# A two-layer hybrid decoder on one core: S5 kernel tables made with swapped operands in four column groups, and the first block's table work emitted later

## Chip, cores, metric

The kernel runs on one core of a Trainium2 chip. The metric is the time of one execution on the device in microseconds, the median of several runs.

## What is computed

256 tokens of width 1024 pass two layers. Each layer has a token mixer of three branches (attention, a spatial gating unit, an S5 state space model), then a feed-forward part: a dense SwiGLU in the first layer, a top-2 of 8 mixture of experts in the second. The S5 branch is the one that is changed here:

```python
dt = jnp.exp(log_dt)[:, None]
lam_bar = jnp.exp(lam * dt)
b_bar = ((lam_bar - 1.0) / lam)[..., None] * b
bu = jnp.einsum('gpi,btgi->btgp', b_bar, u)
_, states = lax.associative_scan(combine, (a, bu), axis=1)
y = jnp.real(jnp.einsum('gip,btgp->btgi', c, states)) + d_skip * u
...
y_c = gelu(y)
y_c = y_c * sigmoid(y_c @ w_glu + b_glu)
```

## The kernel before

Weights stream from HBM and are split on chip into a high and a low part (`wh` on ScalarE, `wl` on VectorE, lines 202 and 203); every product of the dense part is three matmuls, lines 297 to 299. The program is a list of units. A unit is 24 such matmuls for most weights (about 2.9 us of TensorE), and the mixer's list is, in order: zv, v, u, q, k, zu (four units each from u on, here k1 to k4, zu1 to zu4), 24 gate units `gt` (g1 to g24), four units p1 (the gating unit's output projection, tile `pp`), two units wg (tile `pg`, the S5 branch's GLU), p0, p2, and the output projection. After the first layer's mixer come the dense FFN's units, then the second layer's mixer, then the experts.

Between units a planner (`Side`, lines 126 to 171) puts in pieces of the branch work. It runs at build time and settles the order of each engine's instructions; an engine executes in that order and waits where an operand isn't there. The work stands in four lanes of Python generators: P (S5 constants and tables, then `s5_prep`, block by block), A (`s5`: the scans), C (gating unit), B (attention). A positive yield is a cost, a negative one a hold on the lane in units' time. `stream` adds `u.us * rate` to a credit (2.57 x 1.4 in the mixer) up to 3.0, takes 1.13 off for every weight split (made three units ahead) and a further 0.6 for each p1 unit, and gives the rest to `advance` behind the unit's matmuls:

```python
    def advance(self, budget, us):                       # line 151
        for k in self.hold:
            self.hold[k] -= us
        spent = 0.0
        while spent < budget:
            live = [k for k, q in self.lanes.items() if q and self.hold[k] <= 0]
            ...
            spent += self._step(min(live, key=PRIO.index))   # PRIO = "ACPB"
```

A unit can name work that must be whole before it (`pre`): `units[-2].pre = (f"s5{l}",)`, line 1060, names S5 for the first wg unit. `stream` then calls `finish` (lines 163 to 171), which emits all that is left of it, whatever the holds, ahead of the unit's matmuls.

S5 is done in four blocks of 128 channels for each layer. `s5_block` (P) makes a block's tables: VectorE writes the input table into `SB` (`cm`, lines 645 to 658), TensorE transposes it (`pt`, line 680) and ScalarE copies it to `bt`; VectorE writes `SC`; then TensorE multiplies `SB` with the padded output coefficients `cp4` (from GpSimd, lines 664 to 671) and adds the skip term: `kk`, lines 687 to 691. Seven ScalarE copies (lines 694, 698) place parts of `kk` in `ST`. There is one `SB`, while `SC` and `ST` exist twice, so a block from the third on waits until the scan two blocks before it is done. `s5_scan` (A) then does a block: `pp` (line 711), a copy to `vt` (718), 14 VectorE instructions (722 to 741), a hold of 3.5, `py` (748 to 751), a copy into U (752). After the fourth block `s5` applies GELU (538), holds 4.0, reorders with a matmul (548, tile py2), copies (551) and splits the result into `gh` and `gl`, which the wg units read. `s5_u` (line 594, tile `pu`) reorders the input before the first block. In layer 0 blocks are made while the mixer runs, and `s5_prep` starts at k1. In layer 1 they are made during the dense FFN and spilled to HBM, and loaded again when the second mixer begins.

Of the kernel before, what the change touches and what calls it, by code (L numbers as in the profile page):

```python
# [14 lines left out]
AF = mybir.ActivationFunctionType  # L15
# [158 lines left out]
class K:  # L174
# [455 lines left out]
    def s5_block(self, l, b, bc):  # L630
        nc = self.nc
        V = nc.vector
        q = slice(16 * l + 4 * b, 16 * l + 4 * b + 4)
        SC, ST = self.SC[b % 2], self.ST[b % 2]
        pr_ = self.g4("s5p")
        t1, t2 = (pr_[:, 256 * i:256 * i + 256].rearrange("p (q m i) -> p q m i", q=4, m=4) for i in range(2))
        cnp = pr_[:, 512:768].rearrange("p (k q i) -> p k q i", k=2, q=4)

        def cm(dst, coef, yr, yi, neg):
            d4 = [dst[:, 512 * i:512 * i + 512].rearrange("p (q m h i) -> p q m h i", q=4, m=4, h=2)  # L640
                  for i in range(2)]
            xr, xi = (z[:, :, q].rearrange("p m q -> p q m")[:, :, :, None].to_broadcast([128, 4, 4, 16])
                      for z in coef)
            yr, yi = (z[:, :, None, :].to_broadcast([128, 4, 4, 16]) for z in (yr, yi))
            V.tensor_tensor(t1, yr, xr, op=OP.mult)
            V.tensor_tensor(t2, yi, xi, op=OP.mult)
            for h in range(2):
                s = slice(64 * h, 64 * h + 64)
                V.tensor_tensor(d4[0][s, :, :, h], t1[s], t2[s], op=OP.subtract)
            yield 1.4  # L650
            V.tensor_tensor(t1, yr, xi, op=OP.mult)
            V.tensor_tensor(t2, yi, xr, op=OP.mult)
            for h in range(2):
                s = slice(64 * h, 64 * h + 64)
                if neg:
                    V.scalar_tensor_tensor(d4[1][s, :, :, h], t1[s], -1.0, t2[s], op0=OP.mult, op1=OP.subtract)
                else:
                    V.tensor_tensor(d4[1][s, :, :, h], t1[s], t2[s], op=OP.add)
            yield 1.4

        bre, bim, cre, cim = (bc[:, 64 * i:64 * i + 64].rearrange("p (q i) -> p q i", i=16) for i in range(4))

        cp4 = self.sp.tile([128, 3, 4, 32], F32, tag="cpad", name="cpad", bufs=1)
        nc.gpsimd.memset(cp4, 0.0)
        for h in range(2):
            s = slice(64 * h, 64 * h + 64)
            nc.gpsimd.tensor_copy(cp4[s, 0, :, 16 * h:16 * h + 16], cre[s])
            nc.gpsimd.tensor_scalar(cp4[s, 1, :, 16 * h:16 * h + 16], cim[s], -1.0, None, op0=OP.mult)
        d = self.cst[:, C_D + 16 * l + 4 * b:C_D + 16 * l + 4 * b + 4, None]
        nc.gpsimd.tensor_tensor(cp4[:, 2], self.ident[:, None, 96:128].to_broadcast([128, 4, 32]),  # L670
                                d.to_broadcast([128, 4, 32]), op=OP.mult)
        yield from cm(self.SB, self.GT, bre, bim, False)
        yield -2.5

        bt = self.g4("bt")
        for i in range(2):
            pt = self.ax("pt")
            for j in range(4):
                s = slice(512 * i + 128 * j, 512 * i + 128 * j + 128)
                nc.tensor.transpose(pt[:, 128 * j:128 * j + 128], self.SB[:, s], self.ident)  # L680
            nc.scalar.activation(bt[:, 512 * i:512 * i + 512], pt, AF.Copy)
            yield 0.1
        yield from cm(SC, self.LT, cre, cim, True)
        yield -2.5

        kk = self.ax("kk")
        nc.tensor.matmul(kk[:, 0:128], self.ident, cp4[:, 2].rearrange("p q i -> p (q i)"), start=True, stop=False)
        for j in range(4):
            o = kk[:, 32 * j:32 * j + 32]
            nc.tensor.matmul(o, self.SB[:, 128 * j:128 * j + 128], cp4[:, 0, j], start=False, stop=False)  # L690
            nc.tensor.matmul(o, self.SB[:, 512 + 128 * j:512 + 128 * j + 128], cp4[:, 1, j], start=False, stop=j == 3)
        t4 = ST.rearrange("p (q l i) -> p q l i", l=4, i=32)
        kk3 = kk[:, 0:128].rearrange("p (q i) -> p q i", i=32)
        nc.scalar.activation(t4[:, :, 3], kk3, AF.Copy)
        for lo in range(3):
            for m in range(lo + 1):
                s = 3 - lo + m
                nc.scalar.activation(t4[32 * m:32 * m + 32, :, lo], kk3[32 * s:32 * s + 32], AF.Copy)
        yield 0.1
        return bt  # L700
# [1127 lines left out]
```

## Time and profile before

| | us |
|---|---|
| median of 3 runs (1605.46 to 1605.67) | 1605.63 |
| the profiled execution | 1605.73 |
| its span, first to last instruction | 1603.8 |
| TensorE busy | 1552.4 (97%) |
| VectorE busy | 1026.7 (64%) |
| ScalarE busy | 781.9 (49%) |
| mean granted TensorE clock | 0.987 |

The times of the runs are the device's for one execution; the span is that of the instructions inside the profiled one. Layer 0's mixer lies between 7 and 270 us, the dense FFN up to 474, layer 1's mixer behind it, and from about 720 us on the experts. In a timeline row stand the start, the duration, engine, line and operation, output and inputs, shapes, how many are joined in the row, and in brackets how long the engine was idle before and what it waited for. Two records of a float32 matmul are its two passes.

### The profile page before, as it was taken

The numbers are of one execution on the slowest core, as the hardware profiler recorded it, in microseconds if no ns is written. First come the engines' busy times: TensorE is split into PE (matmuls) and PEld (weight loads), VectorE is DVE, ScalarE is ACT, GpSimd is POOL, SyncE is SP. The second block draws the span as 40 slices with busy tenths as digits, with TensorE's granted clock in tenths as the row PEclk, the third lists the DMA queues.
The fourth block names the chain that finished last, engine by engine and source line by source line (L and its number), as shares of the span: only waits on it lengthen the run. The fifth ranks groups of instructions, "written<-read, shape, count | busy, mean of one in ns | idle before, by whom it ended". The sixth has DMA issues, their size and how long they took to land. (4 is left out here: it accounts for less than half of the span.)

```text
span 1603.8 us, 24314 instructions
## 1 busy us (share of the span) xinstructions
PE 1552.4 (97%) x9175; PEld 1178.0 (73%) x9175; DVE 1026.7 (64%) x1501; ACT 781.9 (49%) x1081; POOL 139.0 (9%) x226
## 2 busy tenths in 40 slices
PE   7899999999999999988999999999999999999995
PEld 6899997999879999976766665565665666566551
DVE  7987778687563675667865564655665565565533
ACT  5355564355534557425654454554553554454530
POOL 2621000631001110010000000000000000000000
PEclk9999999999999999998999999999999999999997
DMA  8333356466755534586899999999999999999992
GB/s 328 134 134 130 106 190 244 158 229 232 286 206 215 195 129 164 193 328 240 342 409 397 415 416 413 415 415 415 414 415 415 414 416 415 415 411 415 415 414 113
DMA packets 90045, 487.29 MB, mean 304 GB/s; under 512 B 10128, under 2 KB 10144, under 8 KB 50752
## 3 DMA queue, kind: packets, MB, share of 16 engines
q1 hardware_dynamic: 83376, 462.46, 73.1%
q0 software_dynamic: 6544, 23.20, 4.1%
q8 instruction: 74, 1.21, 0.3%
q14 instruction: 51, 0.42, 0.1%
HBM read 477.23 MB, written 8.39 MB: 303 GB/s over the span
## 5 line engine op out<-in xcount | busy, mean ns | idle before, releaser
L1512 PE MATMUL gu<-moe_u,xes 128*64 128x512 f32 x400 | 165.1, 597 | 0.0
L1512 PE MATMUL gu<-moe_g,xes 128*64 128x512 f32 x400 | 165.0, 597 | 0.0
L203 DVE TENSOR_TENSOR wl<-moe_d,wh 128x1024 fp32r<-128x1024 f32 x112 | 132.6, 1220 | 49.9 <-ACT wh L202 39.5
L203 DVE TENSOR_TENSOR wl<-moe_g,wh 128x1024 fp32r<-128x1024 f32 x112 | 132.0, 1221 | 33.3 <-ACT wh L202 30.6
L203 DVE TENSOR_TENSOR wl<-moe_u,wh 128x1024 fp32r<-128x1024 f32 x112 | 133.9, 1221 | 25.1 <-ACT wh L202 19.4
L202 ACT ACTIVATE wh<-moe_u 128x1024 fp32r<-128x1024 f32 x112 | 116.3, 1058 | 19.5 <-PE moe_g L307 13.8
L202 ACT ACTIVATE wh<-moe_g 128x1024 fp32r<-128x1024 f32 x112 | 116.2, 1058 | 18.4 <-PE da L307 12.3
L202 ACT ACTIVATE wh<-moe_d 128x1024 fp32r<-128x1024 f32 x112 | 113.2, 1052 | 11.7 <-DMA moe_d<-moe_d 7.1
L297 PE MATMUL gt<-XTH,wh 128*128 128x256 f32 x384 | 111.2, 290 | 0.0
L298 PE MATMUL gt<-XTL,wh 128*128 128x256 f32 x384 | 108.5, 283 | 0.0
L299 PE MATMUL gt<-XTH,wl 128*128 128x256 f32 x384 | 108.5, 283 | 0.0
L1512 PEld LDWEIGHTS gu<-moe_g,xes 128*64 128x64 f32 x400 | 46.7, 137 | 78.2 <-issue 74.5
L202 ACT ACTIVATE thl<-pht 128x512 fp32r<-128x512 f32 x28 | 16.7, 597 | 158.9 <-PE pht L1538 158.4
L306 PE MATMUL moe_g<-wh,xeh 128*128 128x512 f32 x224 | 90.9, 406 | 0.0
L306 PE MATMUL da<-wh,thl 128*128 128x512 f32 x224 | 90.5, 404 | 0.0
L307 PE MATMUL moe_u<-wl,xeh 128*128 128x512 f32 x224 | 87.4, 390 | 1.4 <-DVE wl L203 1.4
L307 PE MATMUL moe_g<-wl,xeh 128*128 128x512 f32 x224 | 87.8, 392 | 0.1
L306 PE MATMUL moe_u<-wh,xeh 128*128 128x512 f32 x224 | 87.5, 391 | 0.0
L307 PE MATMUL da<-wl,thl 128*128 128x512 f32 x224 | 87.4, 390 | 0.0
L308 PE MATMUL da<-wh,thl 128*128 128x512 f32 x224 | 87.4, 390 | 0.0
L308 PE MATMUL moe_g<-wh,xel 128*128 128x512 f32 x224 | 87.2, 389 | 0.0
L308 PE MATMUL moe_u<-wh,xel 128*128 128x512 f32 x224 | 87.2, 389 | 0.0
(507 smaller groups left out, 4049.2 us busy)
## 6 DMA issues: line engine op xcount, KB each, us to landing
moe_g<-moe_g SPq DMA_DIRECT2D x68, 1024.0 KB, 12.5
moe_u<-moe_u SPq DMA_DIRECT2D x68, 1024.0 KB, 12.5
moe_d<-moe_d SPq DMA_DIRECT2D x68, 1024.0 KB, 13.5
gt<-w_st SPq DMA_DIRECT2D x24, 1024.0 KB, 4.8
moe_d<-moe_d SPq DMA_DIRECT2D x44, 512.0 KB, 12.2
fw<-ffn_gu SPq DMA_DIRECT2D x18, 1024.0 KB, 4.9
moe_u<-moe_u SPq DMA_DIRECT2D x34, 512.0 KB, 10.5
moe_g<-moe_g SPq DMA_DIRECT2D x34, 512.0 KB, 10.2
```

The source lines that it names most:

```text
L202: self.nc.scalar.activation(h, src, AF.Copy)
L203: self.nc.vector.tensor_tensor(l, src, h.bitcast(F32), op=OP.subtract)
L297: mm(o, wh[:, s], xh[:, x], start=k == 0, stop=False)
L298: mm(o, wh[:, s], xl[:, x], start=False, stop=False)
L299: mm(o, wl[:, s], xh[:, x], start=False, stop=k == nk - 1)
L306: mm(o, xh[:, xs[k]], wh[:, ws[k]], start=first and k == 0, stop=False)
L307: mm(o, xh[:, xs[k]], wl[:, ws[k]], start=False, stop=False)
L308: mm(o, xl[:, xs[k]], wh[:, ws[k]], start=False, stop=last and k == n - 1)
L1512: nc.tensor.matmul(box[0][o:o + 64], x[0][:, 64 * k:64 * k + 64], w[:, 512 * j:512 * j + 512], start=k == 0, stop=k == 7)
```

## The change

`kk` was the product with `SB` as stationary operand (128 columns loaded) and `cp4` as moving one (32 columns). Now `cp4` is stationary (32 columns) and `SB`, or the identity for the skip term, is moving (128 columns); the four groups of states go to four column groups of the array, 32 output partitions each. The result is the transpose of what is wanted, so ScalarE copies it into the unused end of the block's scratch tile and TensorE transposes it back, after a hold of 1.3, into another part of the same PSUM tile. In layer 0's first block alone, the hold ahead of `pt` goes from 2.5 to 7.0 and the hold ahead of `kk` from 2.5 to 5.0.

```diff
         yield from cm(self.SB, self.GT, bre, bim, False)
-        yield -2.5
+        yield -2.5 if l or b else -7.0
...
         yield from cm(SC, self.LT, cre, cim, True)
-        yield -2.5
-
-        kk = self.ax("kk")
-        nc.tensor.matmul(kk[:, 0:128], self.ident, cp4[:, 2].rearrange("p q i -> p (q i)"), start=True, stop=False)
-        for j in range(4):
-            o = kk[:, 32 * j:32 * j + 32]
-            nc.tensor.matmul(o, self.SB[:, 128 * j:128 * j + 128], cp4[:, 0, j], start=False, stop=False)
-            nc.tensor.matmul(o, self.SB[:, 512 + 128 * j:512 + 128 * j + 128], cp4[:, 1, j], start=False, stop=j == 3)
+        yield -2.5 if l or b else -5.0
+
+
+        kt = self.ax("kk")
+        for i in range(3):
+            for j in range(4):
+                w = self.ident if i == 2 else self.SB[:, 512 * i + 128 * j:512 * i + 128 * j + 128]
+                nc.tensor.matmul(kt[32 * j:32 * j + 32, 0:128], cp4[:, i, j], w, start=i == 0, stop=i == 2)
+        kts = pr_[:, 768:896]
+        nc.scalar.activation(kts, kt[:, 0:128], AF.Copy)
+        yield 0.1
+        yield -1.3
+        kk = kt[:, 128:256]
+        nc.tensor.transpose(kk, kts, self.ident)
         t4 = ST.rearrange("p (q l i) -> p q l i", l=4, i=32)
-        kk3 = kk[:, 0:128].rearrange("p (q i) -> p q i", i=32)
+        kk3 = kk.rearrange("p (q i) -> p q i", i=32)
```

## Rows read from the trace of the kernel before

**Rows 1.** Page: span; TensorE's busy tenths in 40 slices of it.
```profile
span 1603.8 us, 24314 instructions
...
PE   7899999999999999988999999999999999999995
```

**Rows 2.** TensorE's waits, 0 to 480 us: total us, times, longest.
```profile
PE pt L680 <- DVE S L649: 3.2, 1, 3.2
```

**Rows 3.** Busy by window: PE, PEld, DVE, ACT, POOL, granted clock, DMA share, GB/s.
```profile
70.00:80.00 10.00, 4.01 (x26) 3.60 (x26) 9.77 (x10) 1.18 (x3) 9.59 (x11) 0.84 0.00 0
```

**Rows 4.** TensorE's timeline from the end of k to the first zu unit.
```profile
71.37 0.28 PE L299 MATMUL k<-XTH,wl 128*128 128x256 f32 x1
74.88 0.63 PE L680 MATMUL pt<-ident,S 128*128 128x128 f32 x4 [3.23 <-DVE S L649]
78.27 1.12 PE L680 MATMUL pt<-ident,S 128*128 128x128 f32 x4 [2.76 <-DVE S L658]
...
79.40 0.42 PE L298 MATMUL zu<-XTL,wh 128*128 128x256 f32 x1
...
83.67 0.30 PE L297 MATMUL zu<-XTH,wh 128*128 128x256 f32 x1
```

**Rows 5.** VectorE's timeline: first block's product, zu's splits, second block's product.
```profile
69.69 1.27 DVE L645 TENSOR_TENSOR s5p<-s5par,GT 128x256 f32<-128x256 f32 x1
...
78.25 2.40 DVE L203 TENSOR_TENSOR wl<-zu,wh 128x1024 fp32r<-128x1024 f32 x2
...
92.35 0.46 DVE L645 TENSOR_TENSOR s5p<-s5par,GT 128x256 f32<-128x256 f32 x1
```

**Rows 6.** TensorE's timeline around the first block's table product.
```profile
87.86 0.28 PE L299 MATMUL zu<-XTH,wl 128*128 128x256 f32 x1
87.97 0.39 PE L687 MATMUL kk<-cpad,ident 128*128 128x128 f32 x2
...
90.10 0.28 PE L298 MATMUL zu<-XTL,wh 128*128 128x256 f32 x1
```

**Rows 7.** TensorE's timeline around `pu`, four column groups of 32.
```profile
52.04 0.28 PE L299 MATMUL q<-XTH,wl 128*128 128x256 f32 x1
...
52.25 1.93 PE L594 MATMUL pu<-uS,ident 128*32 128x256 f32 x32
...
54.33 0.28 PE L298 MATMUL q<-XTL,wh 128*128 128x256 f32 x1
```

**Rows 8.** TensorE's timeline around the third block's eight transpose passes.
```profile
148.10 0.28 PE L299 MATMUL gt<-XTH,wl 128*128 128x256 f32 x1
148.22 1.03 PE L680 MATMUL pt<-ident,S 128*128 128x128 f32 x8
...
149.22 0.28 PE L298 MATMUL gt<-XTL,wh 128*128 128x256 f32 x1
```

**Rows 9.** ScalarE's timeline: fourth block's `vt`, U and GELU.
```profile
191.30 0.60 ACT L718 ACTIVATE vt<-pp 128x512 f32<-128x512 f32 x1
...
208.34 0.37 ACT L752 ACTIVATE U<-py 128x256 f32<-128x256 f32 x1
...
210.02 1.06 ACT L538 ACTIVATE U<-U 128x1024 f32<-128x1024 f32 x1
```

**Rows 10.** VectorE's timeline: fourth block's scan, first and last step; `gl`.
```profile
191.93 0.42 DVE L724 TENSOR_TENSOR tq<-vt,ct 128x256 f32<-128x256 f32 x1
...
198.74 0.42 DVE L741 TENSOR_TENSOR vt<-tq 128x256 f32<-128x256 f32 x1
...
215.90 1.23 DVE L203 TENSOR_TENSOR gl<-yc,gh 128x1024 fp32r<-128x1024 f32 x1 [0.29 <-ACT gh L202]
```

**Rows 11.** TensorE's timeline: fourth block's `py`, py2, the first reader of `gl`.
```profile
202.55 0.33 PE L748 MATMUL py<-U,S 128*128 128x64 f32 x2
...
211.71 1.93 PE L548 MATMUL py<-U,ident 128*32 128x256 f32 x32
...
217.48 0.28 PE L298 MATMUL pg<-gl,wh 128*128 128x256 f32 x1
```

## The prediction

> **What bounds the kernel now.** I read the head of the page first: TensorE is busy eight tenths or more of every slice of the span but the first and the last [rows 1], so a microsecond taken from or put before TensorE in the two mixers or the dense FFN is a microsecond of the whole. Then TensorE's list of waits over the first 480 us: the S5 transposes `pt` stand in it [rows 2], and between 85 and 260 us it has no wait at all. The window of 70 to 80 us shows what happens at that place [rows 3]: TensorE works 4.01 of 10 us, VectorE and GpSimd nearly all of it, and the granted clock is down to 0.84 on the mean. TensorE's timeline there [rows 4] shows three losses: 3.23 us until the first four passes of `pt`, 2.76 us until the other four, and then half speed (1.2 of 2.4 GHz: matmuls 0.41 us long instead of 0.28) up to 83.67 us.
>
> Without them the first unit of zu would have begun at 71.49 (last k matmul 71.37 + 0.12) + 0.88 (eight `pt` passes, below) = 72.4 us; its 22nd matmul would have started 21 x 0.12 = 2.5 us later, at 74.9. It started at 83.67. So the place costs 8.8 us in all, and that is the most that later emission can give back.
>
> **Part 1, the table product.** Before, one block's `kk` is 18 records (9 fp32 matmuls of two passes each), every one with its own load of 128 weight columns, 0.11 us apart on the mean. From the last zu matmul ahead of it (87.86) to the second one behind it (90.10) is 2.24 us [rows 6]; two ordinary steps of 0.12 would be there anyway, so `kk` costs 2.0 us of TensorE, in each of eight blocks.
> The new form is 12 matmuls, 24 passes, of 128 moving columns into four column groups of 32. The trace has this form with 256 columns, in `pu` [rows 7]: 32 passes from 52.25 to 54.33 less the step behind, 2.29 - 0.24 = 2.05 us counted in the same way. A lone 128-column fp32 pass takes 0.11 us: eight transposes `pt` add 1.12 - 0.24 = 0.88 us [rows 8], so a 256-column pass would take 0.22, and 32 of them one by one 7 us. They took 2.05: four run side by side, 8 sets x 0.216 = 1.73, and 0.32 for entering and leaving this form. With 128 columns I take 6 sets x 0.108 + 0.32 = 0.97 us. The added transpose is two passes, 0.22. Saving per block: 2.0 - 0.97 - 0.22 = 0.81 us, in eight blocks 6.5 us. Bounds: if a set doesn't get shorter with fewer columns, 6 x 0.216 + 0.32 + 0.22 = 1.84, saving 1.3 us in all; if the change of form costs nothing, 9.1 us. I take the middle because a pass's time followed its columns [rows 7, 8]. One after another (2.6 + 0.2 us, a loss) is excluded [rows 7].
> The Trainium skill ("TensorE: Matmul & The Clock Gate", section "Wait - 56ns, not 53.3ns?") speaks against this: it says that without hardware decode the sequencer spends about 62 ns on every matmul, however small. By that 24 passes would take 1.5 us and the saving would be near 0.2 us a block, an estimate from that page; by it `pu` would take 2.0 us, and its 32 passes, over within 1.93 us with the last one's end [rows 7], speak against it but not by much.
> The copy `kts` on ScalarE is one more small activation a block, and the transpose stands one unit (2.9 us of TensorE) later, so ScalarE hides it as long as it is less than a unit behind; if not, the price is part of a microsecond at that block. In the FFN blocks nothing else hangs on it: the spilled tables are read over thirty units later.
>
> **Part 2, the first block later.** The planner counts in units: after each unit's matmuls `advance` takes 2.57 off every hold and spends a budget of at most 3.0 - 1.13 = 1.87 on lanes in the order A, C, P, B. A hold of 2.5 or 1.3 thus lasts one unit, 5.0 two, 7.0 three. I went through the units with these numbers (zu1 to zu4, then gate units g1 to g24, then p1-1 to p1-4, then wg1). For the kernel before, this count gives `pt` behind k4, `kk` behind zu2, the last block's `py` behind p1-1, `py2` behind p1-3: so it stands in the trace [rows 4, 6, 11]. As block: pt, kk, pp, py:
> before 0: k4, zu2, zu3, g3; 1: g3, g6, g7, g11; 2: g12, g14, g15, g19; 3: g18, g20, g21, p1-1.
> after 0: zu2, g1 (transpose g3), g4, g8; 1: g8, g12 (g13), g14, g18; 2: g17, g19 (g20), g21, p1-1; 3: g24, p1-2 (p1-3), p1-4, and `py` no longer before wg1.
>
> At the first block: zu1 now follows k4 at once, 71.49 to 74.4, then the attention scores. But zu2 needs its low half `wl`, and VectorE does that only behind the S5 product for this block, at 78.25 + 1.2 = 79.45 [rows 5]. That product is slow because GpSimd is busy then (1.27 us for what takes 0.46 at 92 us [rows 5]), which the change doesn't touch. So a wait for `pt` becomes a wait of some 4 us for `wl`. Then zu2's 22 other matmuls to 82.1 and `pt` to 83.0; before, both were done at 87.98 [rows 6]. Gain 5.0 us if the clock stays, 3.0 if it falls as it did before (20 steps took 4.27 us instead of 2.4 [rows 4]). I take 3.5; bounds 2 and 8.8.
>
> **Part 3, what comes due too early.** `wg1` may not start before S5 is done (`pre`). Before, its inputs were only just there: `gl` ended at 215.90 + 1.23 = 217.13, the matmul that reads it started at 217.48 [rows 10, 11]. After, the fourth block's `pp` stands behind p1-4, the last unit ahead of wg1, and `finish` puts the rest of S5 in front of wg1. TensorE executes in order, so it waits out this chain:
> - `vt` copy 0.60 [rows 9];
> - the scan on VectorE from 191.93 to 198.74 + 0.42 = 7.2 us, with one weight split in it, as there will be after [rows 10];
> - the rest of `py`, 20 of 24 passes at 0.11 [rows 6] and the last one's end: 2.5;
> - copy of U and GELU with its table load, 208.34 to 211.08: 2.7 [rows 9];
> - `py2` 1.93 [rows 11];
> - copies, `gh`, `gl`: at most 217.13 - 213.64 = 3.5 [rows 10, 11]; one weight split stood in it, I take 3.0.
> Sum 17.9. TensorE had to do `py` (24 x 0.11 = 2.7) and `py2` (2.05) anyway, so it idles 13.2 us, 13.5 with the `mg` product of p1-4 that VectorE does in the same queue. It idles 7 us at a stretch, longer than before the clock's fall above [rows 4], so the clock falls: `py` at half speed +2.1, `py2` +1.7, the start of wg1 +1.9, as 4.27 less 2.4 above. I take 4.5 of these 5.7. Loss 18.0 us, bounds 13.2 and 19.5. Nothing gives it back: behind it come units on which TensorE is busy without waits.
> Layer 1's reload begins at m1[0], over thirty units behind the last spill, so its chain doesn't move.
>
> **Sum.** Profiled execution 1605.73 (span 1603.8 + 1.9 around it; the median of the runs is 0.1 lower): -6.5 - 3.5 + 18.0 = +8.0, so 1613.7, against the median 1613.6 us.
>
> **Rivals.**
> A, faster: S5 of layer 0 still reaches `gh` ahead of wg1. Then part 3 is nothing and the time is 1605.6 - 10.0 = 1595.6. It decides at one point: `py` of block 3 must stand two units before wg1 (the hold of 4.0 ahead of `py2`). For it: the lanes share one budget, and attention ends three units earlier in my count. Against: the count, which fits the trace of before at every place I compared.
> B, the product isn't cheaper: the sets of four stay at 0.216, the saving is 1.3 us and the time 1618.8. By the 62 ns a matmul that the Trainium skill states (same page and section) it would be about 1618, an estimate.
> C, a draw: TensorE's saving is at its upper bound (9.1), VectorE's splits come in time at the first block (up to 8.8), and the clock holds at the end (13.5 to 18): within 3 us of before.
> D, a new wait: block 1's `pt` stands two units behind its product on VectorE (g6 and g8), where before five units lay between; if VectorE is late as at block 0, about 3 us more: 1616.6.
>
> **How the numbers follow.** The forecast 0.60, A 0.12, B 0.12, C 0.06, D 0.10. 0.2%, 3.2 us, is about what a measurement here tells from no change. Faster 0.12 (A), same 0.07 (C, and the edge of the forecast), slower 0.81. The forecast's own range: low end -9.1 - 5 + 15.5 = +1.4, high end -1.3 - 2 + 19.5 = +16; both at once are unlikely. I give 1604.5 to 1620, which leaves out A and the far ends of B and D.
>
> **What would show it.** A `wl` in place of `S` as what TensorE waits for near 76 to 80 us, about 4 us. The table product in about 1 us of TensorE from step to step, its transpose a unit later without a wait. Near 212 to 235 us two or three new waits ahead of `pg` (on VectorE's `vt`, on ScalarE's U, on `gh` or `gl`) of some 13 us together and half clock there. FFN stretches 0.8 us shorter for each block. I am wrong in kind if TensorE goes from p1-4 into wg1 with no gap (A), and in size if the clock holds through the gap.

## The result, and the profile after

The changed kernel takes 1614.67 us (median of 5 runs, 1613.08 to 1614.95), the kernel before beside it 1605.46 (1604.24 to 1605.67): a ratio of 1.0059, 95% interval 1.0048 to 1.0070. It is slower by 9.2 us. The forecast was 1613.6. The profiled execution took 1614.82 us. In the experiments below one execution of the kernel before (4155 us) and one of the kernel with the transpose beside `pp` (3927 us) took more than twice as long as the others; ranges and ratios leave them out.

The page of after, its span, TensorE's busy tenths and its granted clock in 40 slices of 40.3 us:

```profile
span 1612.7 us, 24444 instructions
...
PE   7999969999999999997999999999999999999995
...
PEclk9999979999999999998999999999999999999997
```

The span is 8.9 us longer than that of [rows 1]. The sixth slice (202 to 242 us) has lost a third of TensorE's work, and the clock, at 9 tenths there before, is down to 7; that is where wg1 stands. The busy time by window shows the two places (columns as in [rows 3]):

```profile
70.00:80.00 10.00, 6.25 (x49) 5.58 (x48) 9.77 (x10) 1.88 (x2) 9.58 (x11) 0.87 0.00 0
...
210.00:220.00 10.00, 4.16 (x19) 3.98 (x19) 6.33 (x14) 0.00 (x0) 0.00 (x0) 0.53 0.30 105
220.00:230.00 10.00, 5.08 (x38) 2.43 (x38) 0.66 (x1) 5.72 (x7) 0.00 (x0) 0.62 0.01 2
230.00:240.00 10.00, 9.38 (x65) 9.38 (x66) 4.70 (x6) 3.40 (x7) 0.00 (x0) 0.83 0.00 0
```

At 70 us TensorE works 6.25 of 10 us where it worked 4.01 [rows 3], beside the same 9.77 of VectorE and 9.58 of GpSimd. From 210 to 240 us it works 18.6 of 30, at a granted clock of 0.53, 0.62 and 0.83.

What TensorE waited for up to 480 us (total, times, longest):

```profile
PE py L757 <- DVE vt L744: 6.9, 1, 6.9
PE zu L299 <- DVE wl L203: 3.7, 1, 3.7
PE py L548 <- ACT U L538: 2.8, 1, 2.8
PE pg L297 <- ACT gh L202: 1.8, 1, 1.8
...
PE pt L681 <- DVE S L658: 1.0, 1, 1.0
PE pg L298 <- DVE gl L203: 0.9, 1, 0.9
...
PE kk L698 <- ACT s5p L694: 0.6, 1, 0.6
...
PE py L758 <- DVE vt L748: 0.6, 1, 0.6
```

The two waits of `pt` in the first block (3.2 [rows 2] and 2.8 [rows 4]) are gone, one for zu's `wl` stands there instead. The five of `py`, py2 and `pg` are new, 13.0 us together; all lie between the last p1 unit and wg1, as TensorE's timeline of that place shows:

```profile
206.23 1.90 PE L718 MATMUL pp<-U,bt 128*128 128x64 f32 x16
207.96 0.39 PE L755 MATMUL py<-U,S 128*128 128x64 f32 x2
215.28 0.69 PE L757 MATMUL py<-vt,S 128*128 128x63 f32 x2 [6.93 <-DVE vt L744]
...
220.42 0.64 PE L758 MATMUL py<-vt,S 128*128 128x63 f32 x2
223.89 3.64 PE L548 MATMUL py<-U,ident 128*32 128x256 f32 x32 [2.84 <-ACT U L538]
229.36 0.38 PE L297 MATMUL pg<-gh,wh 128*128 128x256 f32 x1 [1.83 <-ACT gh L202]
230.62 0.39 PE L298 MATMUL pg<-gl,wh 128*128 128x256 f32 x1 [0.88 <-DVE gl L203]
...
234.06 0.41 PE L297 MATMUL pg<-gh,wh 128*128 128x256 f32 x1
...
234.61 0.28 PE L297 MATMUL pg<-gh,wh 128*128 128x256 f32 x1
```

The fourth block's `pp` stands behind p1-4 and the rest of S5 behind it, then wg1. Behind the long wait a pair of `py` passes takes 0.64 us or more, where the first pair, still at full speed, takes 0.39 and [rows 11] has 0.33; py2 takes 3.64 instead of 1.93 [rows 11]: half speed. The clock was at 1.2 GHz from 210.6 to 227.7 us, and once more from 231.1 to 234.5, behind the two waits of `pg`. By the time of the same matmul in both traces, the distance grows by 25.85 us from p1-4 (203.27) to the steady part of `pg` (234.61). 6.4 of these are work that before did earlier (`pp` 1.76, `py` 2.6, py2 2.05). So the place costs 19.4 us: 13.0 of waits, about 5.5 of half speed (`py` 2.3, py2 1.7, the start of wg1 1.5), and 0.9 in which the last matmul ahead of a wait runs to its end.

The first block, where zu2's third matmul now waits:

```profile
75.15 0.28 PE L298 MATMUL zu<-XTL,wh 128*128 128x256 f32 x1
79.18 0.58 PE L299 MATMUL zu<-XTH,wl 128*128 128x256 f32 x1 [3.75 <-DVE wl L203]
79.56 0.42 PE L297 MATMUL zu<-XTH,wh 128*128 128x256 f32 x1
...
84.04 1.17 PE L681 MATMUL pt<-ident,S 128*128 128x128 f32 x8
84.96 0.36 PE L297 MATMUL zu<-XTH,wh 128*128 128x256 f32 x1
```

zu2 runs at 0.21 us a step behind its wait, half speed, to 84 us. zu3 begins at 84.96, in before at 89.90 with the 2.0 us of `kk` done. That is 2.9 us earlier, of which 0.4 were there from 28 us on, ahead of anything changed: a gain of 2.5 us.

And the new table product with its transpose, between gate units:

```profile
96.54 0.28 PE L299 MATMUL gt<-XTH,wl 128*128 128x256 f32 x1
96.75 0.64 PE L692 MATMUL kk<-S,cpad 128*32 128x128 f32 x16
97.21 0.40 PE L692 MATMUL kk<-ident,cpad 128*32 128x128 f32 x8
97.54 0.39 PE L297 MATMUL gt<-XTH,wh 128*128 128x256 f32 x1
97.76 0.28 PE L298 MATMUL gt<-XTL,wh 128*128 128x256 f32 x1
...
104.49 0.28 PE L299 MATMUL gt<-XTH,wl 128*128 128x256 f32 x1
104.61 0.27 PE L698 MATMUL kk<-ident,s5p 128*128 128x128 f32 x1
104.64 0.36 PE L297 MATMUL gt<-XTH,wh 128*128 128x256 f32 x1
104.84 0.28 PE L298 MATMUL gt<-XTL,wh 128*128 128x256 f32 x1
```

Counted as in the prediction (from the last matmul ahead to the second behind, less two steps), the product takes 97.76 - 96.54 - 0.24 = 0.98 us, the transpose 104.84 - 104.49 - 0.24 = 0.11: together 1.1 us against 2.0.

### The profile page after: what moved, and what is told of

The parts are those of the page before. It is cut to its first block, busy times and chain, and to the rows that moved or that the text cites. A ratio compares the mean times of both kernels' runs of the same rounds, so it can differ in the third digit from the quotient of the medians.

```text
span 1612.7 us, 24444 instructions
## 1 busy us (share of the span) xinstructions
PE 1549.8 (96%) x9231; PEld 1172.8 (73%) x9231; DVE 1025.9 (64%) x1501; ACT 785.7 (49%) x1091; POOL 133.7 (8%) x226
```

## Experiments

Times are medians; the kernel before, run beside them, took 1604.43 us (first four), 1604.66 (next four) and 1604.47 (the last).

### The holds alone

```diff
-        yield -2.5
+        yield -2.5 if l or b else -7.0
...
-        yield -2.5
+        yield -2.5 if l or b else -5.0
```

> The kernel before with only the first block's two holds changed (7.0 and 5.0), the table product as it was. Theory (S5 comes due at wg1): by the count py of block 3 stands behind p1-4, GELU's, py2's and gh's work is forced ahead of wg1; TensorE waits there for GELU (2.8 us) and for gh and gl (2.7 us), 5.5 us, and up to 3 more if the clock falls; the first block gives back 2.5. Time 1608.5 to 1611.5. Rival (the new table product and its extra copy are what costs): the first block's 2.5 us are a plain gain, 1603.

Measured: 1616.63 us (1614.89 to 1616.8), 1.0073 [1.0060, 1.0087]. The sign is the theory's, the size is not: 5 us more. The wait for zu's `wl` is there, 3.8 us, and the first block gains 2.4. At wg1 TensorE waits 5.3 us (U 2.8, `gh` 1.8, `gl` 0.7) and is at half clock from 218.6 to 232.2 us; the place costs 9.8 us. What the expectation hadn't is the second block, TensorE's timeline:

```profile
122.83 1.01 PE L680 MATMUL pt<-ident,S 128*128 128x128 f32 x4 [2.04 <-ACT sT L872]
123.50 0.56 PE L297 MATMUL gt<-XTH,wh 128*128 128x256 f32 x1
123.86 0.41 PE L298 MATMUL gt<-XTL,wh 128*128 128x256 f32 x1
```

The second half of block 1's `pt` waits, and the wait is paid twice: 2.0 us, and half speed for the unit behind it, to 126.4 us; 4.3 us in all. The place is rival D's, the reason is not: VectorE had written this block's `SB` by 107.3 us. The bracket names ScalarE's copy `sT` of the attention's transposes. These transposes, `py` and `pt` take turns in one ring of four PSUM tiles (`ax`), and counted by turns the second `pt` needs the tile that the first of the two `sT` copies (122.3 us on) empties. ScalarE came to them late, after 8.9 us of idling for VectorE's `zv`.

### The swapped product alone

The change without the two lines above: holds of 2.5 everywhere, the product and the transpose (with its hold of 1.3) as in the change.

> The change's table product with its copy, hold of 1.3 and transpose, but the first block's holds at 2.5 as before. Theory: each block is one unit later, so py of block 3 is again forced ahead of wg1, but its scan is long done: waits of 5.5 us there as in the run with the holds alone, up to 3 more for the clock; the product saves 6.5; the first block's wait for pt stays. Time 1604.5 to 1607.5. Rival (the product's own form costs): near 1612 to 1615. Rival (nothing comes due, the product alone): 1599.

Measured: 1606.02 us (1605.31 to 1607.96), 1.0011 [1.0002, 1.0020], as expected. The waits of `pt` are those of before. The product is cheaper, and yet nothing is gained: at wg1 there are waits of 2.8 (U), 1.8 (`gh`), 0.8 (`vt`) and 0.7 us (`gl`), and half clock from 212.5 to 226.1 us. So each half of the change by itself makes S5 late for wg1, the one by its holds, the other by the unit that its transpose stands later in each block.

### The swapped product, its transpose beside `pp`

The product as in the change, all holds as before; in layer 0 the transpose has no hold of its own but is emitted with the `pp` pass of its block, before `py` needs its result.

```diff
         nc.scalar.activation(kts, kt[:, 0:128], AF.Copy)
         yield 0.1
-        yield -1.3
-        kk = kt[:, 128:256]
-        nc.tensor.transpose(kk, kts, self.ident)
+        def place():
+            kk = kt[:, 128:256]
+            nc.tensor.transpose(kk, kts, self.ident)
...
+        if l == 0:
+            self.kkp[b] = place
+            return bt
+        yield -1.3
+        place()
```

> Swapped product as in the change, first block's holds as before, and in layer 0 no hold for the transpose: it and the copies into ST are issued right behind the block's pp, one unit after the product, so that every unit's order is that of the kernel before. Theory: nothing comes due early, no wait ahead of wg1, eight products at 0.8 us less: 1599 (1597.5 to 1600.5). Rival (the product's form or the copy on ScalarE costs): 1605 or more.

Measured: 1594.25 us (1593.44 to 1594.34), 0.9936 [0.9923, 0.9949], 4.7 us better than expected and outside the interval given. The window at wg1 has no idle time left:

```profile
210.00:220.00 10.00, 10.00 (x87) 9.83 (x84) 7.70 (x10) 7.09 (x12) 0.00 (x0) 1.00 0.58 210
```

By the time of the same matmul in both traces each block of layer 0 gains 0.95 to 1.08 us, and the four of the dense FFN 3.0: 7.2 us up to its end at 400 us, where 8 x 0.81 had been foreseen. Another 4 us come around 700 us in layer 1, where this edit changes no instruction; the experiment with the router load, below, is about that.

### wg free of S5

The change, but layer 0's wg units don't name S5 as their `pre` and read other tiles of the same shape (the low and high half of the gating unit's output, and `zu` in the last step). All of S5 is still done; its result in layer 0 goes unused.

```diff
-                    self.prod_st(o[:, 256 * t:256 * t + 256], wh, wl, 4, 256, 128 * t, *self.gin)
+                    self.prod_st(o[:, 256 * t:256 * t + 256], wh, wl, 4, 256, 128 * t, *(self.gin if l else self.yb))
...
-        units[-2].pre = (f"s5{l}",)
+        units[-2].pre = (f"s5{l}",) if l else ()
```

> The changed kernel, but in layer 0 the wg units read the gating unit's result instead of S5's and don't wait for S5, which is finished behind them (its result is then not used: that part of the output is left out). The work on every engine is the same. Theory: the loss at wg1, 13 us of waits and about 6 of half speed, is gone: 1614.7 - 19.3 = 1595.4 (1593 to 1598). Rival (the loss is spread over many places): 1605 or more.

Measured: 1597.75 us (1596.63 to 1598.13), 0.9957 [0.9944, 0.9971], as expected. The changed kernel loses its whole slowdown and 7 us more with one dependency. In the window where the change has 4.16 of 10 us and 0.53 there is

```profile
210.00:220.00 10.00, 10.00 (x86) 10.00 (x84) 8.61 (x14) 4.86 (x10) 0.00 (x0) 1.00 0.35 113
```

From 1614.67 it is 16.9 us; each against the kernel before beside it, 15.9 (9.2 slower, 6.7 faster). The 19.4 us counted on the trace are more because this kernel loses 3.0 us of its own while the rest of S5 is done beside later units (by the same matmuls, up to the end of layer 0's mixer), 1.7 of them in waits for `wl` at the output projection that the change has not.

The same edit in the kernel before is the control:

> Control: the kernel before with layer 0's wg units reading the gating unit's result and not waiting for S5 (S5's result is then not used, that part of the output is left out), as was done to the changed kernel. Theory (before, S5 is in time and nothing is lost at wg1): no change, 1603.5 to 1605.5. Rival (freeing wg gives something by itself): 1601 or less, and then as much less of the 17 us between the changed kernel and its freed form belongs to S5 coming due.

Measured: 1603.87 us (1602.2 to 1605.0), 0.9998 [0.9988, 1.0007]. In the kernel before, S5 is in time for wg1 and the dependency costs nothing.

### GpSimd's last work ahead of the product moved behind it

The kernel before, in which the first block's two last GpSimd table levels (not needed by the first block's input table) are emitted behind the VectorE product into `SB`, so that VectorE and GpSimd don't work at once there. Two copies of one column of `SB` stand ahead of them and make GpSimd wait for the product (1.24 and 1.19 us on GpSimd).

```diff
-        for k in range(6):
...
+        def rest():
+            G.tensor_copy(tmp[:, 0:1], self.SB[:, 1023:1024])
+            G.tensor_copy(tmp[:, 512:513], self.SB[:, 1023:1024])
+            levels((4, 5))
+        levels(range(6) if l else range(4))
+        self.rest = rest
...
         yield from cm(self.SB, self.GT, bre, bim, False)
+        if l == 0 and b == 0:
+            self.rest()
```

> The kernel before with one thing changed: GpSimd's two largest steps of layer 0's tables (levels 4 and 5) wait until VectorE has finished the first block's input table, instead of running beside it. No hold is changed. Theory (the first block's loss comes from VectorE's product being slowed to 1.2 us an instruction while GpSimd works beside it): the product's eight instructions take about 3.5 us instead of 8.5 and end near 72 us, TensorE's 6 us of waits for the block's transposes shrink to 1 or less, its clock stays, 7 to 8.5 us come back: 1596 to 1597.5 against 1604.4. Rival (VectorE is late because of its own queue): 1603 to 1605.

Measured: 1599.29 us (1598.14 to 1601.08), 0.9966 [0.9952, 0.9979]: a gain, but 2 to 3 us less than expected. VectorE's timeline, the first product and the same kind of work some 10 us later:

```profile
68.12 0.42 DVE L652 TENSOR_TENSOR s5p<-s5par,GT 128x256 f32<-128x256 f32 x1
...
78.19 2.03 DVE L663 SCALAR_TENSOR_TENSOR S<-s5p 64x256 f32<-64x256 f32 x2
80.26 1.96 DVE L203 TENSOR_TENSOR wl<-zu,wh 128x1024 fp32r<-128x1024 f32 x1
```

and TensorE's, which comes from k to `pt` with no wait:

```profile
71.32 0.28 PE L299 MATMUL k<-XTH,wl 128*128 128x256 f32 x1
71.44 1.04 PE L689 MATMUL pt<-ident,S 128*128 128x128 f32 x8
```

The product step takes 0.42 us instead of 1.27 [rows 5], and by the end of zu1 TensorE is 8.8 us ahead: the 8.8 us that the prediction gave as the price of the whole place is its price. But GpSimd's work has only moved. It now runs beside the table `SC` (73.8 to 80.2 us) and zu's split (1.96 us instead of 1.2), and two gate units wait for `wl`, 2.8 us together, with half clock from 96.0 to 99.4: 4.7 us go back.

### Router load first

The kernel before, with one statement moved: in layer 1 the router's constants (32 KB, a DMA on GpSimd's queue) are requested ahead of the normalisation's and the residual's loads, not behind them.

```diff
         def wo_pre():
+            if l == 1:
+                self.route_consts()
             self.ln_params(l, 0)
...
-            if l == 1:
-                self.route_consts()
```

> The kernel before, but in layer 1 the router's 32 KB load is the first of the loads ahead of the output projection instead of the last. The kernel before waits 1.8 us there for a ScalarE split that stands behind the split of the router's weights, and runs 3.4 us at half speed; the changed kernel and the run with the transpose at pp show no such wait. Theory (this is where 3 us of their gain in layer 1 come from, chance of one late load): 1604.4 - 3 = 1601.4 (1600.5 to 1602.5). Rival (the wait has another cause): 1604.4, no change.

Measured: 1600.33 us (1599.62 to 1601.58), 0.9975 [0.9965, 0.9984], 0.2 us below the range of the theory and far from its rival. What it takes away is in ScalarE's waits of the kernel before, 680 to 760 us:

```profile
ACT rhl L202 <- DMA rc<-rt: 4.5, 1, 4.5
```

ScalarE waits 4.5 us in its order for that load; behind it stand the weight splits of the output projection, and TensorE waits for one of those, and then goes at half clock from 701.5 to 704.9 us (TensorE's waits of before, 600 to 760 us):

```profile
PE wo L306 <- ACT wh L202: 1.8, 1, 1.8
...
PE wo L307 <- DVE wl L203: 0.8, 1, 0.8
```

Before's list of DMA issues has the load at 16.4 us from issue to landing. Four loads of 512 KB are requested ahead of it on the same queue, the last two those of `z`, and weight loads of 1 MB run on another queue meanwhile:

```profile
z<-scr_x POOLq DMA_DIRECT2D x2, 512.0 KB, 15.1
rc<-rt POOLq DMA_DIRECT2D x1, 32.0 KB, 16.4
```

Requested first, it lands after 5.3 us, and neither ScalarE's wait nor TensorE's for `wh` is in the lists any more. After's list has it at 14.6:

```profile
rc<-rt POOLq DMA_DIRECT2D x1, 32.0 KB, 14.6
```

In after, ScalarE's wait is down to 2.7 us, and TensorE's wait for `wh` and the half clock behind it are gone, as in the kernel with the transpose beside `pp`.

### Product, transpose and GpSimd together; and with the router load

The transpose beside `pp` and GpSimd's work moved behind, in one kernel:

> The swapped product with its transpose beside pp (the kernel of the run with the transpose at pp, 1594.25) and GpSimd's two largest table steps behind the first block's product. Theory: both gains add, 1594.3 - 7.5 = 1586.8 (1585.5 to 1588.5). Rival (GpSimd's tables come too late for the first scan, TensorE waits at py of block 0): 1590 or more.

Measured: 1591.23 us (1590.41 to 1592.84), 0.9919 [0.9906, 0.9933]. It beats both kernels, but is 2.7 us above the expectation's range. That had taken 7.5 us for GpSimd's move, which alone gave 5.4. By the same matmuls this kernel is 10.9 us ahead at the end of the dense FFN, and the two edits alone are 7.0 and 4.2: up to there they add but for 0.4 us. The number is in the rival's range, but TensorE does not wait at `py` of block 0. `pp` of the first block now comes early, and the transpose beside it waits 2.9 us for ScalarE's copy (TensorE's timeline), with half speed behind it to 91.0 us. That costs 4.8 us, in place of the 4.7 that the waits for `wl` cost with GpSimd's move alone:

```profile
87.74 0.47 PE L708 MATMUL kk<-ident,s5p 128*128 128x128 f32 x1 [2.91 <-ACT s5p L703]
87.87 0.56 PE L297 MATMUL zu<-XTH,wh 128*128 128x256 f32 x1
88.23 0.42 PE L298 MATMUL zu<-XTL,wh 128*128 128x256 f32 x1
```

With the router load first as well:

> Three edits in one kernel: the swapped table product with its transpose beside the pp pass in layer 0 (first block's product later, holds of S5 as before), the first block's two GpSimd copies emitted behind the cmSC step, and the router's constants requested first in layer 1. The first two together took 1591.2, and that kernel's layer 1 no longer had the output projection waiting for a weight cast. Theory that the router load is already off the path there: 1590.0 to 1592.0, no difference from the two. Rival that the load still costs part of its 3 to 4 us in layer 1: 1588.0 to 1590.0.

Measured: 1590.19 us (1589.24 to 1591.72), 0.9913 [0.9899, 0.9926]. The intervals of the two overlap, and without this edit the load landed after 13.5 us and TensorE did not wait for `wh`: what the router load costs is already off the path there.

## Why the prediction came out as it did

The time was 1.1 us above the forecast, for the reason forecast: part 3. But the terms of the sum were less good than the sum. Measured on the trace, they are

| | predicted | measured |
|---|---|---|
| first block later (part 2) | -3.5 | -2.5 |
| table product (part 1), with the waits it brought | -6.5 | -4.7 |
| S5 due at wg1 (part 3) | +18.0 | +19.4 |
| layer 1 | 0 | -3.3 |
| sum | +8.0 | +8.9 |

The span grew by 8.9; 0.4 us gained at the start and 0.4 lost again behind the router's load stand beside the table and cancel. That the sum came so near is in good part luck: the first three terms were off by 1.0, 1.8 and 1.4 us, all to the slow side, and layer 1, which stood in no term, took 3.3 back.

**The order of the work** came as the count had it, at every place of the table: `pt` behind zu2, `kk` behind g1, its transpose behind g3, and at the end `pp` behind p1-4. That count carries the prediction's sign, and with it rival A fell: the point it named, `py` of block 3 two units before wg1, was missed: nearly all of that `py` was still to come when wg1 was due.

**Part 3.** The idle time was right, 13.0 us against 13.2 (13.5 with `mg`), and so were the links of the chain: the copy 0.60, the scan 7.6 (7.2 foreseen), U and GELU 2.7, the split of the result 3.0. The term that was mis-sized is the clock: 5.7 us had been worked out for `py`, py2 and wg1's start at half speed, and 4.5 were taken. It cost about 5.5, and 0.9 more went into the ends of the last matmuls ahead of the waits, of which the forecast had counted one. The discount had no row behind it. The kernel with wg free of S5 shows the cause: without that one dependency 16 to 17 us are gone, and in the kernel before the same dependency costs nothing.

**Part 1.** The product was forecast at 0.97 us and took 0.98: a pass's time does follow its columns, and rival B fell. The rule weighed there, that without hardware decode the sequencer spends about 62 ns on every matmul (the Trainium skill, "TensorE: Matmul & The Clock Gate", section "Wait - 56ns, not 53.3ns?"), does not set the pace here: the 24 passes lie between 96.75 and 97.61 us, under 36 ns each. How the matmuls were decoded, no run here shows. The transpose was taken as two passes and is one, 0.11 us. That could have been read beforehand: the loop at line 680 issues eight transposes a block, and [rows 8] has eight records. So a block saves 0.9 us or more, where 0.81 was foreseen; undisturbed, with the transpose beside `pp`, eight blocks saved 7.2 us. The change gets 4.7 of that. In layer 0 it is 1.8: the second block's `pt` waits 1.0 us (rival D's wait, at a third of its price), and about 1 us I could not place. In the FFN it is 2.85, with one transpose waiting 0.6 us for ScalarE's copy, as the text allowed.

**Part 2.** The wait for `wl` came where it was put, 3.7 us for "some 4", and the clock fell as it had before. For that case the text had 3.0 us, and 2.9 came, 2.5 when the 0.4 us from the start are taken off. The 3.5 leaned towards a clock that holds, although the rows showed it falling behind a wait of that size [rows 4].

**Layer 1** is the step that failed. "Nothing gives it back" was said from the list of waits up to 480 us. Further on the kernel before has waits of 1.8 and 0.8 us and 3.4 us of half clock, which go back to one small load on a crowded queue. The kernel with the router load first shows that this costs 4.3 us; by the same matmuls the changed kernel is spared 3.3 of them without any edit there, the one with the transpose beside `pp` about 4, and even the control, whose layer 1 is that of before, 2.4. TensorE's wait for `wh` goes with the landing of the load: 1.8 us at 16.4 (before), 1.3 at 15.9 (GpSimd later), 0.9 at 15.5 (the holds alone, the control), none at 14.6 (after) and 13.7 (the transpose beside `pp`). Why the load lands earlier in one kernel than in another stays open, and with one trace of each it isn't shown how far it differs from execution to execution. Without this gift the change would have been some 12 us slower, and the forecast 4 too low.

## What to carry to other kernels

A cheaper operation that adds a link to a dependent chain is paid at the chain's deadline: here 7 us of TensorE were to be had, and one transpose a unit later in each block cost more than that, while the same transpose, put beside the next pass of its block, brought no wait there. Look up what is due at the end of the lane, and count its slack in units before counting what is saved. And read the list of waits over the whole span: a wait that the change doesn't touch can still go away when everything ahead of it moves.

## What the runs showed of the hardware

Matmuls into four column groups of 32 outputs ran side by side: 24 passes of 128 columns in 0.86 us from the first start to the last end, where 24 passes one by one would take 2.6 by estimate (at 0.11, [rows 6]).

The granted clock made short waits dear. At or behind waits of TensorE of 2.0 us (the holds alone), 2.4 (GpSimd later), 2.9 (product and GpSimd together) and 3.7 (after, at zu2) it stood at 1.2 instead of 2.4 GHz for some 3.4 us or more, and so it did behind pairs of 1.8 and 0.8 or 0.9 us close together (before, at `wo`; after, at `pg`). Behind those of 1.0 us (`pt`) and 0.6 (`kk`) in after it did not fall. After the 6.9 us at `py` it stayed low for 17 us, 210.6 to 227.7, while TensorE worked on with gaps.

VectorE beside GpSimd took 1.27 us for an instruction that takes 0.42 alone [rows 5, 10], and moving GpSimd's work moved the slowness to whatever stood there.
